# A hybrid decoder layer: small transfers on another queue, later gates, earlier reloads, and pairs that begin with a plain unit

## The chip, the cores and the metric

The kernel runs on one core of a Trainium2 chip. The metric is the device time of one execution in microseconds. The median of three runs before the change is 2062.15 us (2055.52 to 2067.89).

The core has a matrix engine (TensorE, PE in the profile), three engines for elementwise work (VectorE = DVE, ScalarE = ACT, GpSimd = POOL) and a queue engine (SyncE = SP). Transfers between memory and the chip are issued by SP, ACT or POOL, each in the order of its own instructions.

## The reference

A batch of 1, 256 tokens and 2048 features pass through one decoder layer in float32:

```python
hn = rmsnorm(h, norm_mix_w)
q, k, v, g_ret, xr, yr, g_a, g_b = split(hn @ w_in)
ret_out = silu(g_ret) * head_groupnorm(chunkwise_retention(rotary(q), rotary(k) * 128**-0.5, v))
rnn_out = gelu(yr) * rg_lru(causal_dwconv(xr), w_a, w_x, lam)
merged = sigmoid(g_a) * (ret_out @ w_proj_ret) + sigmoid(g_b) * (rnn_out @ w_proj_rnn)
h = h + merged @ w_mix_out
h = h + cross_attention(rmsnorm(h), rmsnorm(mem), w_q, w_k, w_v, w_o)   # 256 memory tokens, 4 heads of 512
u = causal_dwconv(rmsnorm(h) @ ffn_w_up)                                # 2 x 5632
h = h + (silu(gate) * val) @ ffn_w_down
return rmsnorm(h, final_norm_w)
```

## The kernel before

**Products.** Every float32 operand is split into a high and a low half that TensorE multiplies exactly, and a product is the sum of three: high by high, low by high, high by low. Activations are kept split (tiles `s`, in groups of two feature tiles); weights are split as they arrive.

**The weight stream.** `weight_plan` lists the blocks of 512 columns in the order of their use; `entry_units` cuts each into units of 4 feature tiles by 512 columns (1 MB). `prefetch` handles one unit: a transfer from `wall` into one of five `raw` buffers on SP (L261), a copy to `hi` by ScalarE (L282, 1.9 us), a subtraction into `lo` by VectorE (L283, 2.3 us). The generator `units` keeps two units split ahead of the matmuls (AHEAD).

**Single blocks and pairs.** `gemm_t` (L342) and `gemm_n` (L352 to L354) multiply one block. `pair_products` (L380 to L383) multiplies two blocks at once, and for the first eight of its 16 feature tiles it uses seven products where eight would be needed (a Strassen-like scheme): seven units `q1` to `q7` of 12 matmuls, and four plain units `p` of 24. Some `q` units work on sums of weights: "add" units are made by an accumulating transfer on POOL into a raw buffer that is already there (L263), a "sum" unit by a VectorE addition of two raw buffers (L287, at `q5`). Their other operand may be `ss`, sums of activations (`sums`, L479 to L485). Order of a pair's units:

```python
q1  p(8-11)  q3  p(12-15)  q5  q2  q6  p(8-11)  p(12-15)  q7  q4
```

where `p(8-11)` reads feature tiles 8 to 11, `p(12-15)` the last four, and `q1` four of the first eight. There are 16 pairs.

**Order of the work.** `later(n, fn)` puts `fn` off until n + 1 more units have been emitted. A framework schedules the program: each engine's instructions are put in an order from priority (the order of the program) and a simulated time at which they are ready, and run in that order.

**Kept tiles.** `Kept` stores finished tiles of `ret`, `rnn` and `qs` (256 KB each, eight of each) to memory and loads them back at the first `[i]`, splitting them, both on POOL (L711, L718). `Pairs` loads tiles of `x_t` and `mem_t` on SP (L607), up to two ahead; `ms` is the memory. `hkept` holds the residual during attention (4 x 512 KB, POOL, L1041 and L1137).

**The stages that the change touches.** (a) `recurrent` runs four times, each with two single blocks, and puts `recur` off: its gates (16 TensorE matmuls at L854 and 16 ScalarE functions for four tiles) in one go after the next unit, then `weigh`, `drive`, `scan`. (b) Three gate pairs (O_GA, O_GA, O_GB) follow; the last recurrence falls into the first. `ret` and `rnn` come back around there. (c) Attention: two pairs on `xa_w_q` whose results are transposed and stored in `qs` by `keep`; two pairs on `xa_w_k`, whose results `turn_key` transposes before `softmax`, two heads each; one pair on `xa_w_v` and two singles, each followed by `attend`. Memory rows `ms[0..3]` are asked for in the second `xa_w_q` pair, `ms[4..7]` in the first two units of the first `xa_w_k` pair; queries `qs[i]` in `turn_key`. (d) The feed-forward: 11 blocks in parts of 4, 4, 3; the first two parts end with two pairs each on `ffn_w_down`, whose 16 feature tiles are the part's hidden tiles, the last of them finished just before.

Of the kernel before, what the change touches and what calls it, by code (L numbers as in the profile page):

```python
# [19 lines left out]
NT = D // P  # L20
# [7 lines left out]
BW = 512  # L28
KC = 4
# [34 lines left out]
def weight_plan():  # L64

    w0 = "w_in"
    plan = []
    for g in range(2):
        for c in (O_Q, O_K):
            plan += [(w0, 0, NT, c + g * BW), (w0, 0, NT, O_V + g * 1024 + (c == O_K) * BW)]  # L70
        plan += [(w0, 0, NT, O_G + g * 1024 + b * BW) for b in range(2)]
    for b in range(4):
        plan += [(w0, 0, NT, c + b * BW) for c in (O_XR, O_YR)]
    for w, c, pairs in ((w0, O_GA, (0, 2)), (w0, O_GB, (0,)), ("w_proj_ret", 0, (0, 2))):
        plan += [(w, 0, NT, c + b * BW, c + (b + 1) * BW) for b in pairs]
        if len(pairs) == 1:
            plan += [(w, 0, NT, c + b * BW) for b in (2, 3)]
    plan += [("w_proj_rnn", 0, NT, b * BW) for b in range(4)]
    plan += residual_plan("w_mix_out")
    plan += [(w, 0, NT, b * BW, (b + 1) * BW) for w in ("xa_w_q", "xa_w_k") for b in (0, 2)]  # L80
    plan += residual_plan("xa_w_v")
    plan += residual_plan("xa_w_o")
    b0 = 0
    for nb_ in FF_PARTS:
        for b in range(b0, b0 + nb_):
            plan += [("ffn_w_up", 0, NT, c + b * BW) for c in (0, FF)]
        if nb_ == 4:
            plan += [("ffn_w_down", b0 * BW, NT, b * BW, (b + 1) * BW) for b in (0, 2)]
        else:
            plan += [("ffn_w_down", b0 * BW, 4 * nb_, b * BW) for b in range(4)]  # L90
        b0 += nb_
    return plan
# [19 lines left out]


def entry_units(e):

    w, row, nk, cols = e[0], e[1], e[2], e[3:]
    if len(cols) == 1:
        return [("p", None, "new", (w, tuple(row + (k + i) * P for i in range(KC)), cols[0])) for k in range(0, nk, KC)]
    out = []
    for kind, slot, a in PAIR_UNITS:  # L120
        if kind == "p":
            out.append((kind, slot, "new", (w, tuple(row + (a[1] + i) * P for i in range(KC)), cols[a[0]])))
        elif a[0] == "sum":
            out.append((kind, slot, "sum", None))
        else:
            out.append((kind, slot, a[0], (w, tuple(row + (2 * i + a[1]) * P for i in range(KC)), cols[a[2]])))
    return out
# [23 lines left out]
def hybrid_layer(  # L151
# [215 lines left out]
    def pair_products(w, row, st, ss, c0, c1, out):  # L367
# [17 lines left out]
        names = {"q1": "x", "q2": "y", "q3": "r", "q4": "u", "q5": "z", "q6": "x", "q7": "x"}  # L385
        for kind, parts in units(w, row, NT, c0, c1):
            if kind == "p":
# [316 lines left out]
    class Kept(list):  # L704
# [4 lines left out]
        def store(self, t):  # L709

            pool.dma_start(out=self.rows[self.stored], in_=t)  # L711
            self.stored += 1

        def __getitem__(self, i):
            while len(self) <= i:
                assert len(self) < self.stored
                t = tmp("kt")
                pool.dma_start(out=t, in_=self.rows[len(self)])  # L718
                self.append(split_pair(t, self.scale))
                if self.summed and len(self) <= KC:  # L720
                    self.sums.append(sums(t, self.scale))
# [125 lines left out]
    def recur(b, rgw, xr, gl):  # L847
        aa, tt_, ti = big([P, 4, S], s="aa"), big([P, 4, S], s="tt"), big([P, 4, S], s="ti")
        for j in range(4):
            t = 4 * b + j  # L850
# [34 lines left out]

        for n, fn in zip((0, 1, 2) if b < 3 else (6, 11, 17), (weigh, drive, scan)):
            later(n, fn)
# [32 lines left out]
    def sum_x(i):  # L920

        t = tmp("xt")
        pool.dma_start(out=t, in_=x_t[:, 2 * i : 2 * i + 2, :])
        for j in range(2):
# [115 lines left out]
    for b in range(4):  # L1040
        pool.dma_start(out=hkept[b], in_=hrow[b])  # L1041

# [48 lines left out]
    for b in (0, 2):  # L1091
        if b == 2:
            for i in range(KC):
                later(2 + 2 * i, lambda i=i: ms[i])
        for i, o in enumerate(pair_out("xa_w_q", h1s, h1s_sums, b * BW)):
            for pr in range(2):
                later(2 * i + pr, lambda o=o, pr=pr: keep(o, pr, qs))
    for i in range(KC):
        later(i // 2, lambda i=i: ms[KC + i])

    def turn_key(b, o, pr, ks):
        for t in transposed(o[:, :, pr * S : (pr + 1) * S]):
            ks.append(split_pair(t))
        qs[2 * b + pr]
        if pr == 1:
            later(1, lambda: softmax([qs[2 * b], qs[2 * b + 1]], ks))

    for b in (0, 2):
        for i, o in enumerate(pair_out("xa_w_k", ms, ms.sums, b * BW, rsms[0])):
            ks = []  # L1110
            for pr in range(2):
                later(3 * i + pr, lambda b=b + i, o=o, pr=pr, ks=ks: turn_key(b, o, pr, ks))
    osp, osp_sums = [], []
# [19 lines left out]
    for i, o in enumerate(pair_out("xa_w_v", ms, ms.sums, 0)):  # L1133
        later(3 * i, lambda b=i, o=o: attend(b, split_rows(o, rsms[0])))
    hrow = [big([P, 2, BW], s="nat") for _ in range(4)]
    for i in range(4):
        pool.dma_start(out=hrow[i], in_=hkept[i])  # L1137
    for b in (2, 3):
# [141 lines left out]
```

## Time and profile before

| | |
|---|---|
| median of 3 runs | 2062.15 us |
| profiled execution, its time | 2058.05 us |
| its span, first to last instruction | 2056.2 us |
| busy: PE, DVE, ACT, POOL | 2018.2, 1496.6, 1128.1, 83.0 us |
| mean granted TensorE clock | 0.991 |
| bytes read and written | 431.45 MB, 10.49 MB |
| SP's queue, POOL's queue | 371.17 MB, 68.16 MB |

Times in views of the trace are microseconds from the start of the span. A row of a group gives line, engine, operation, tiles, count, busy time and idle time before it with what ended it. A wait "A <- B: t, n, m" says that A waited for B t us in all, n times, at most m. In the chain of waits, a row is what the end of the kernel hung on at that moment. A row of transfers ends with the median time from issue to landing.

### The profile page before, as it was taken

To read this page: it belongs to the slowest core of one execution; us is meant where nothing else is said; L and a number is where in the kernel's file an instruction comes from. 1 tells how busy PE (TensorE), PEld (TensorE's weight loads), DVE (VectorE), ACT (ScalarE), POOL (GpSimd) and SP (SyncE) were. 2 spreads that over 40 slices of the span, in tenths; PEclk is the share of its full clock that TensorE was granted. 3 is DMA by queue.
4 is the path that set the end of the run, shared out by engine and by line. 5 is a ranking of instruction groups with operands and counts; after the bars stand their busy time and mean duration, and the time that the engine had idled before them with its cause. 6 is when DMAs were issued, how large, how long until landed. Compare 5 with 4: busy or idle time off the path is not lost.

```text
span 2056.2 us, 24973 instructions
## 1 busy us (share of the span) xinstructions
PE 2018.2 (98%) x10120; PEld 1708.9 (83%) x10120; DVE 1496.6 (73%) x1535; ACT 1128.1 (55%) x1143; POOL 83.0 (4%) x120
## 2 busy tenths in 40 slices
PE   9999999999999999999899899999999999999998
PEld 8888888888788888888787788888878888788887
DVE  6747657988775776777776667578778687776765
ACT  6445447766565554565655555555454555454543
POOL 0000000000100000000100000000000000000000
PEclk9999999999999999999899999999999999999999
DMA  9554554565887775887967757555569555685552
GB/s 365 209 213 181 188 195 160 215 209 156 267 285 254 227 267 193 256 282 236 292 205 219 236 164 226 185 192 192 188 185 279 185 202 192 165 278 213 184 205 82
DMA packets 74403, 443.56 MB, mean 216 GB/s; under 512 B 8496, under 2 KB 13232, under 8 KB 25008
## 3 DMA queue, kind: packets, MB, share of 16 engines
q1 hardware_dynamic: 60544, 371.17, 48.8%
q0 software_dynamic: 12224, 68.16, 15.3%
q10 hardware_dynamic: 1520, 2.63, 0.4%
q8 instruction: 79, 1.29, 0.2%
q14 instruction: 36, 0.29, 0.0%
HBM read 431.45 MB, written 10.49 MB: 215 GB/s over the span
## 4 chain that ended last, share of the span: by engine, by line
PE 84%; DVE 5%; DMA 5%; ACT 3%; issue 2%; POOL 0%; SPq 0%; POOLq 0%; DVEq 0%; ACTq 0%
PE acc L342 34%; PE acc L354 8%; PE acc L352 8%; PE acc L353 8%; PE acc L383 8%; PE acc L380 8%; PE acc L382 8%; DVE lo L283 3%; DMA raw<-in_wall 2%; PE sm L496 2%; ACT hi L282 1%; DMA xt<-in_mem_t 1%; DMA kt<-qs 1%; PE sm L508 1%; DVE raw L287 0%
## 5 line engine op out<-in xcount | busy, mean ns | idle before, releaser
L283 DVE TENSOR_TENSOR lo<-raw,hi 128x2048 fp32r<-128x2048 f32 (+1 forms) x408 | 923.0, 2269 | 425.1 <-ACT hi L282 424.0
L282 ACT CAST hi<-raw 128x2048 fp32r<-128x2048 f32 (+1 forms) x406 | 769.7, 1901 | 672.3 <-PE acc L353 175.8
L342 PE MATMUL acc<-s,hi 128*128 128x512 f32 x2176 | 520.0, 392 | 1.5 <-DVE hi L280 0.9
L342 PEld LDWEIGHTS acc<-s,hi 128*128 128x128 f32 x2176 | 402.5, 189 | 81.6 <-issue 1.4
L352 PE MATMUL acc<-hi,s 128*128 128x512 f32 (+1 forms) x760 | 292.6, 385 | 0.0
L354 PE MATMUL acc<-lo,s 128*128 128x512 f32 (+1 forms) x760 | 291.4, 383 | 0.0
L353 PE MATMUL acc<-hi,s 128*128 128x512 f32 (+1 forms) x760 | 291.1, 383 | 0.0
L342 PEld LDWEIGHTS acc<-s,lo 128*128 128x128 f32 x2176 | 278.4, 192 | 11.0 <-DVE lo L283 1.9
L380 PE MATMUL acc<-hi,s 128*128 128x512 f32 x704 | 279.2, 397 | 7.3 <-ACT hi L282 4.3
L342 PE MATMUL acc<-s,lo 128*128 128x256 f32 x2176 | 284.3, 284 | 1.1 <-DVE lo L283 1.1
L383 PE MATMUL acc<-lo,s 128*128 128x512 f32 x704 | 278.3, 395 | 5.2 <-DVE lo L283 5.0
L382 PE MATMUL acc<-hi,s 128*128 128x512 f32 x704 | 278.1, 395 | 1.1 <-DVE s L553 1.1
L354 PEld LDWEIGHTS acc<-lo,s 128*128 128x128 f32 x760 | 142.9, 188 | 28.2 <-DVE lo L283 0.2
L353 PEld LDWEIGHTS acc<-hi,s 128*128 128x128 f32 x760 | 143.0, 188 | 27.2 <-DVE s L530 0.2
L352 PEld LDWEIGHTS acc<-hi,s 128*128 128x128 f32 x760 | 143.0, 188 | 27.0 <-ACT s L529 0.3
L380 PEld LDWEIGHTS acc<-hi,s 128*128 128x128 f32 x704 | 133.9, 190 | 37.4 <-ACT hi L282 6.2
L383 PEld LDWEIGHTS acc<-lo,s 128*128 128x128 f32 x704 | 134.0, 190 | 36.9 <-DVE lo L283 9.6
L382 PEld LDWEIGHTS acc<-hi,s 128*128 128x128 f32 x704 | 134.0, 190 | 30.0 <-DVE s L553 1.9
L380 PE MATMUL acc<-hi,ss 128*128 128x512 f32 x256 | 101.7, 397 | 0.9 <-ACT o L434 0.4
L383 PE MATMUL acc<-lo,ss 128*128 128x512 f32 x256 | 100.5, 392 | 0.1
L382 PE MATMUL acc<-hi,ss 128*128 128x512 f32 x256 | 99.9, 390 | 0.0
L263 POOL DMA_DIRECT2D raw<-in_wall x48 | 41.9, 873 | 1086.3 <-DVE lo L283 765.8
(243 smaller groups left out, 1422.5 us busy)
## 6 DMA issues: line engine op xcount, KB each, us to landing
raw<-in_wall SPq DMA_DIRECT2D x337, 1024.0 KB, 4.9
raw<-in_wall POOLq DMA_DIRECT2D x48, 1024.0 KB, 9.3
raw<-in_wall SPq DMA_DIRECT2D x5, 512.0 KB, 8.5
nat<-in_x ACTq DMA_DIRECT2D x4, 512.0 KB, 10.5
ret<-hd POOLq DMA_DIRECT2D x8, 256.0 KB, 6.5
rnn<-rn POOLq DMA_DIRECT2D x8, 256.0 KB, 4.2
kt<-ret POOLq DMA_DIRECT2D x8, 256.0 KB, 8.3
kt<-rnn POOLq DMA_DIRECT2D x8, 256.0 KB, 5.5
```

What stands on the lines that cost most here:

```text
L263: pool.dma_start(out=raw, in_=src, accum_op=ALU.add)
L282: act.copy(hi[:, a:b], raw[:, a:b])
L283: dve.tensor_tensor(out=lo[:, a:b], in0=raw[:, a:b], in1=hi[:, a:b].bitcast(F32), op=ALU.subtract)
L342: pe.matmul(a, part, sx, start=k == 0 and t == 0, stop=k == nk - 1 and t == 0, skip_group_check=True)
L352: pe.matmul(o, h, hi, start=start, stop=False)
L353: pe.matmul(o, l, hi, start=False, stop=False)
L354: pe.matmul(o, h, lo, start=False, stop=stop)
L380: pe.matmul(o[0], h, hi, start=o[1] not in begun, stop=False, skip_group_check=True)
L382: pe.matmul(o[0], l, hi, start=False, stop=False, skip_group_check=True)
L383: pe.matmul(o[0], h, lo, start=False, stop=kk == KC - 1, skip_group_check=True)
L496: pe.matmul(o, a, b, start=start and i == 0, stop=stop and i == 2, skip_group_check=True)
L508: pe.transpose(t[:, j, tt * P : (tt + 1) * P], rows[:, tt, k + j * P : k + (j + 1) * P], ident)
```

## The change

- The stores and loads of `Kept`, the `x_t` tiles of `sum_x`, and `hkept`'s stores and loads are issued by SP in place of POOL. The accumulating weight transfers stay on POOL.
- `recur` puts its four gate tiles off singly: two after the first unit, two after the second; `weigh`, `drive`, `scan` follow two units later than before in the first three recurrences.
- Three of the 16 pairs carry a flag in the plan: the first O_GA pair, and the first `ffn_w_down` pair of each of the two full parts. A flagged pair takes its units in the order `p(8-11) q1 p(12-15) q3 q2 q5 q6 p p q7 q4`; the weight stream follows.
- `ms[0]` and `ms[1]` are asked for in the first `xa_w_q` pair, `ms[2..7]` in the second.
- `qs[0..3]` are asked for after units 5, 7, 9 and 11 of the first `xa_w_k` pair, `qs[4..7]` in the second, and no longer in `turn_key`.
- `keep`, `turn_key` and the first two `attend` come one unit later.

```diff
-        plan += [(w, 0, NT, c + b * BW, c + (b + 1) * BW) for b in pairs]
+        plan += [(w, 0, NT, c + b * BW, c + (b + 1) * BW) + (True,) * (c == O_GA and b == 0) for b in pairs]
...
-            plan += [("ffn_w_down", b0 * BW, NT, b * BW, (b + 1) * BW) for b in (0, 2)]
+            plan += [("ffn_w_down", b0 * BW, NT, b * BW, (b + 1) * BW) + (True,) * (b == 0) for b in (0, 2)]
...
+PLAIN_FIRST = [PAIR_UNITS[i] for i in (1, 0, 3, 2, 5, 4, 6, 7, 8, 9, 10)]
...
-    w, row, nk, cols = e[0], e[1], e[2], e[3:]
+    w, row, nk, cols = e[0], e[1], e[2], e[3:5]
...
-    for kind, slot, a in PAIR_UNITS:
+    for kind, slot, a in PLAIN_FIRST if e[5:] else PAIR_UNITS:
...
-        for kind, parts in units(w, row, NT, c0, c1):
+        e = (w, row, NT, c0, c1)
+        for kind, parts in units(*e, *plan[gemms[0]][5:]):
...
-            pool.dma_start(out=self.rows[self.stored], in_=t)
+            sp.dma_start(out=self.rows[self.stored], in_=t)
...
-                pool.dma_start(out=t, in_=self.rows[len(self)])
+                sp.dma_start(out=t, in_=self.rows[len(self)])
...
-        for j in range(4):
+
+        def gates(j):
...
-        for n, fn in zip((0, 1, 2) if b < 3 else (6, 11, 17), (weigh, drive, scan)):
+        for j in range(4):
+            later(j // 2, lambda j=j: gates(j))
+        for n, fn in zip((2, 3, 4) if b < 3 else (6, 11, 17), (weigh, drive, scan)):
...
-        pool.dma_start(out=t, in_=x_t[:, 2 * i : 2 * i + 2, :])
+        sp.dma_start(out=t, in_=x_t[:, 2 * i : 2 * i + 2, :])
...
-        pool.dma_start(out=hkept[b], in_=hrow[b])
+        sp.dma_start(out=hkept[b], in_=hrow[b])
...
-        if b == 2:
-            for i in range(KC):
-                later(2 + 2 * i, lambda i=i: ms[i])
+        for i in range(KC):
+            if b == 0 and i < 2:
+                later(5 + 4 * i, lambda i=i: ms[i])
+            elif b == 2:
+                later(2 * i, lambda i=i: ms[i])
+                later(9 + i // 2, lambda i=i: ms[KC + i])
...
-                later(2 * i + pr, lambda o=o, pr=pr: keep(o, pr, qs))
-    for i in range(KC):
-        later(i // 2, lambda i=i: ms[KC + i])
+                later(1 + 2 * i + pr, lambda o=o, pr=pr: keep(o, pr, qs))
...
-        qs[2 * b + pr]
...
+        for i in range(KC):
+            later(4 + 2 * i, lambda i=i: qs[2 * b + i])
...
-                later(3 * i + pr, lambda b=b + i, o=o, pr=pr, ks=ks: turn_key(b, o, pr, ks))
+                later(1 + 3 * i + pr, lambda b=b + i, o=o, pr=pr, ks=ks: turn_key(b, o, pr, ks))
...
-        later(3 * i, lambda b=i, o=o: attend(b, split_rows(o, rsms[0])))
+        later(1 + 3 * i, lambda b=i, o=o: attend(b, split_rows(o, rsms[0])))
...
-        pool.dma_start(out=hrow[i], in_=hkept[i])
+        sp.dma_start(out=hrow[i], in_=hkept[i])
```

## The prediction

> **What bounds the kernel now.** I read the page first: which engine is full, and what is left of the span.
>
> ```profile
> span 2056.2 us, 24973 instructions
> PE 2018.2 (98%) x10120; PEld 1708.9 (83%) x10120; DVE 1496.6 (73%) x1535; ACT 1128.1 (55%) x1143; POOL 83.0 (4%) x120
> PEclk9999999999999999999899999999999999999999
> ```
>
> TensorE is busy 98% of the span, so no edit beside it can shorten the work. What can go is the time in which it stands or runs at a lower granted clock. To find that I cut the span into stages. A stage is one weight block (a "single", or a "pair" of blocks made of 11 units and 180 matmuls); its bounds come from the matmul counts in the timeline. The view by windows gives length, PE busy and the matmul count of each. Columns: window, length, busy and count of PE, PEld, DVE, ACT, POOL, then the granted clock, DMA share, GB/s.
>
> ```profile
> 334.90:361.00 26.10, 26.10 (x148) 22.74 (x146) 19.29 (x24) 20.73 (x34) 1.64 (x3) 1.00 0.58 211
> 361.00:384.10 23.10, 22.53 (x130) 19.66 (x129) 23.10 (x33) 13.29 (x16) 1.63 (x3) 1.00 0.61 226
> 410.20:433.40 23.20, 22.55 (x130) 19.76 (x129) 21.62 (x32) 12.46 (x15) 1.65 (x3) 1.00 0.68 238
> 481.90:529.30 47.40, 45.63 (x198) 36.38 (x197) 37.64 (x34) 36.66 (x41) 3.98 (x6) 1.00 0.65 200
> 529.30:576.00 46.70, 43.13 (x181) 34.69 (x181) 36.41 (x34) 25.46 (x19) 5.36 (x8) 0.96 0.87 266
> 660.50:701.40 40.90, 40.90 (x181) 33.72 (x180) 28.42 (x16) 24.83 (x19) 1.96 (x3) 1.00 0.72 223
> 920.90:963.90 43.00, 42.62 (x190) 34.30 (x189) 30.43 (x22) 25.39 (x24) 3.92 (x5) 1.00 0.74 234
> 963.90:1007.70 43.80, 43.15 (x198) 35.22 (x197) 37.04 (x39) 31.28 (x34) 4.04 (x7) 1.00 0.94 288
> 1007.70:1061.30 53.60, 48.83 (x197) 38.52 (x196) 35.71 (x28) 29.75 (x30) 7.27 (x11) 0.87 0.79 249
> 1061.30:1118.40 57.10, 52.34 (x253) 43.77 (x252) 38.73 (x37) 30.45 (x34) 4.87 (x8) 0.94 0.68 203
> 1118.40:1176.20 57.80, 52.33 (x253) 43.66 (x252) 39.24 (x37) 30.62 (x35) 4.43 (x7) 0.94 0.74 225
> 1228.80:1272.90 44.10, 44.06 (x205) 36.27 (x204) 31.15 (x20) 24.17 (x17) 1.71 (x2) 1.00 0.67 204
> 1498.90:1543.60 44.70, 42.05 (x182) 33.39 (x181) 36.35 (x32) 24.51 (x21) 1.71 (x2) 1.00 0.66 201
> 1762.50:1807.00 44.50, 42.21 (x183) 33.47 (x183) 36.36 (x32) 24.61 (x21) 1.75 (x2) 1.00 0.66 201
> ```
> The chain of waits has the undisturbed single (start us, us, what):
> ```profile
> 53.35 22.22 PE acc L342 x128
> ```
>
> The measure of a pair that nothing disturbs is 40.9 us (660.50); a unit of it is 12 matmuls, 2.7 us, and a plain unit 24 matmuls, 5.4 us. The pair at 1228.80 has 24 more small matmuls and takes 3.2 us more, so one costs 0.13. Its neighbours are measured against that:
>
> - Pairs on xa_w_k and xa_w_v at 1061.30 and 1118.40: 72 small ones, 9.4 us. Lost: 57.1 - 40.9 - 9.4 = **6.8**, and **7.5**.
> - First xa_w_k pair at 1007.70: 16 small ones, 2.1. Lost: 53.6 - 40.9 - 2.1 = **10.6**.
> - The xa_w_q pairs: 43.0 - 40.9 - 1.0 = 1.1, and 43.8 - 40.9 - 2.1 = 0.8.
> - First two gate pairs at 481.90 and 529.30: 94.1 less 81.8, less the recurrence's 16 gate matmuls (26.1 - 22.2 = 3.9, first row). Lost: **8.4**.
> - First ffn_w_down pairs: **3.8** and **3.6**.
> - Two stages behind recurrences (361.00, 410.20): 0.9 and 1.0.
>
> About 44 us in all: no change to the waits can bring more. Now what ended last in the worst of them, from the chain of waits, SP's timeline and VectorE's timeline:
>
> ```profile
> 1011.14 9.59 DMA xt<-in_mem_t
> ...
> 1083.26 0.56 POOL raw L263
> 1083.82 12.95 DMA kt<-qs
> 1096.80 0.63 ACT s L526
> ...
> 1140.99 13.62 DMA kt<-qs
> ```
> ```profile
> 1001.12 9.93 SPq L261 DMA_DIRECT2D raw<-in_wall  x3
> 1011.14 2.22 SPq L607 DMA_DIRECT2D xt<-in_mem_t  x3
> ```
> ```profile
> 529.08 0.29 DVE L479 TENSOR_TENSOR sm<-kt 128x128 f32<-128x128 f32 x1 [1.59 <-DMA kt<-ret]
> 534.32 0.29 DVE L479 TENSOR_TENSOR sm<-kt 128x128 f32<-128x128 f32 x1 [2.14 <-DMA kt<-ret]
> ...
> 1509.64 0.69 DVE L530 SCALAR_TENSOR_TENSOR s<-fo,s 128x512 fp32r<-128x512 f32 x1
> ...
> 1512.44 0.69 DVE L530 SCALAR_TENSOR_TENSOR s<-fo,s 128x512 fp32r<-128x512 f32 x1
> ```
>
> At 1083.8 a query reload leaves GpSimd right behind an accumulating weight load, lands 13 us later, and softmax's matmuls wait for its split; the same at 1141.0. At 1001-1011 SyncE's queue stood before three weight loads, and the last three memory rows left only then. The clock adds to each: it is granted at half for 13.6 us there and for 6.8 us behind the first query wait.
>
> ```profile
> 1013.60:1027.20 13.60, 10.79 (x28) 7.80 (x29) 6.67 (x10) 5.25 (x12) 3.85 (x7) 0.50 1.00 368
> 1095.50:1102.30 6.80, 4.83 (x20) 4.51 (x21) 4.41 (x5) 4.70 (x4) 0.00 (x0) 0.50 0.45 178
> ```
>
> **The change, part by part.**
>
> *Queries a block ahead: -12.3.* Before, a query was asked for two or three units ahead of its softmax (turn_key after unit 1 + 3i + pr, softmax two units on): 8 to 14 us against 13 us of transfer. Now query i of the pair of heads is asked for after unit 5 + 2i of the pair before, the last with unit 11, and softmax of the head that needs it comes after units 5 and 8 of the next. That leaves eight units or more, 30 us. The splits (0.63 us on ScalarE, about as much on VectorE) move with it, four into the pair at 1007.70, whose VectorE loses four memory splits in exchange. I leave 1.0 us per pair, as in the xa_w_q pairs, which have no such wait: -5.8 - 6.5 = -12.3. Bounds: 0 if the reload still lands late, -14.3 if all goes.
>
> *Memory rows earlier, transposes one unit later: -6.1.* The last four memory pairs were asked for after units 1 and 2 of the xa_w_k pair that uses the first of them in its unit 2. Now it is units 10 and 11 of the pair before: 5.4 and 8.2 us earlier; two more go to the first xa_w_q pair. The transfers then land at 1013 to 1015 instead of 1020.7, against 1010.4 when unit 2 begins. 3 to 5 us of wait stay, with a little of the low clock: I leave 4.5 of 10.6. Transposes of a result (keep, turn_key, attend) come one unit later, so that they no longer stand right behind VectorE's last add. Bounds: 0, and -9.6 with 1.0 left.
>
> *First gate pair begins plain, gates two tiles per unit: -2.9, and -0.9 at the recurrences.* The plain unit gives the splits 5.4 us in place of 2.7 at the start, and ScalarE gets eight of its 16 gate functions a unit later. But the two waits of VectorE above (1.59 and 2.14) are for kept rows, which the change doesn't bring earlier; I leave 5.5 of 8.4 and half of 1.9. Bounds: 0 and -7.4; 0 and -1.9.
>
> *First ffn_w_down pairs begin plain: +2.0.* Old order: q1, plain 8-11, q3, plain 12-15, so the plain unit that reads the last two hidden tiles begins 2.7 + 5.4 + 2.7 = 10.9 us in. New order: plain, q1, plain: 8.2 us in, at 1507.0. Those tiles' splits end at 1510.3 and 1513.1 (rows at 1509.64 and 1512.44), and VectorE's timeline shows no gap from 1500 to there. The wait is 3.3, then four to six matmuls, then 1.4: 4.7 against the 3.8 and 3.6 lost now, as the later stalls of the pair are taken in by it: +0.9 and +1.1. Bounds: -2.8 each if the scheduler puts those splits first, +4 each if the clock falls too.
>
> *Small transfers on SyncE's queue: 0.* 60 move: 8 stores and 8 loads each of ret, rnn and qs, 4 of x_t, 8 of hkept. Waits and landings in the profile:
>
> ```profile
> SPq L261 <- DVE lo L283: 1690.6, 312, 19.8
> ```
> ```profile
> xt<-in_mem_t SPq DMA_DIRECT2D x8, 256.0 KB, 10.1
> kt<-qs POOLq DMA_DIRECT2D x8, 256.0 KB, 12.1
> xt<-in_x_t SPq DMA_DIRECT2D x7, 256.0 KB, 7.9
> xt<-in_x_t POOLq DMA_DIRECT2D x4, 256.0 KB, 5.1
> ```
>
> SyncE issues in order and waits most of the span for VectorE to free a raw buffer. A store that waits for VectorE stands in the same order as VectorE's own instructions, so it adds little; a load waits for the weight loads ahead. GpSimd keeps the 48 accumulating loads and loses what stood before them. The cover is the lead of two split units before the matmuls, 5.4 us or more. The price without it is the second rival's. Bounds: that rival, and -3.7 (1.59 + 2.14) if kept rows land in time.
>
> The Trainium skill, "SBUF — State Buffer", section "SBUF: two separate sides", says that transfers issued from GpSimd starve for descriptors while VectorE runs certain copies, and that SP's run at full speed. By it those 3.7 us would go, and the sum be 3.7 lower. The rows don't bear it out: the same x_t tile took 5.1 us from GpSimd and 7.9 from SyncE. I go by the rows.
>
> **Sum.** -12.3 - 6.1 - 2.9 - 0.9 + 2.0 = -20.2. The profiled execution took 2058.05 us, 1.85 over its span: 2037.9. The median of the three runs, 2062.15, lies 4.1 above it (2055.52 to 2067.89); I add half of that: **2040**.
>
> **The rivals.**
>
> 1. *The queries aren't early in fact.* They are asked for on SyncE, where a load goes behind weight loads that wait for buffers: the memory rows stood 9.9 us so. If the reloads are held until the pair that uses them, -12.3 falls away: -7.9, that is 2050, with the median's 2 about 2052; up to 2060 if the other steps do half. For it: the SyncE rows above. Against: 30 us of lead against 10 of waiting and 10 of landing.
>
> 2. *Slower: VectorE stands before rows that SyncE brings late.* VectorE runs in order; a split of a kept row set before a weight's lo half holds that half, and TensorE with it. This is what the pair at 1007.70 shows: memory rows on SyncE, 10.6 lost. 16 reloads of ret and rnn fall into the three gate pairs and after, 8 of qs into the pairs at 1007.70 and 1061.30. If the gate pairs each lose 10.6 (31.8 against 8.4 now: +23.4) and the three attention pairs too (31.8 against 24.9: +6.9), with +2.0 and -0.9: +31.4, 2091. It decides as soon as a small load lands more than two units (5.4 us) after its place in VectorE's order. The Trainium skill, "DMA: Bandwidth & Descriptors", section "Anatomy of one DMA — SWDGE (gpsimd) path", has the rule behind it: a wait is held on the issuing sequencer, before dispatch. SyncE's 1690.6 us of waiting agree.
>
> 3. *More goes.* All bounds on the good side but the ffn ones: -14.3 - 9.6 - 7.4 - 1.9 = -33.2, 2025, with the median's 2: 2027; to 2018 with the ffn gain and the kept rows.
>
> **How the numbers follow.** A measurement of this kernel tells about 0.5%, 10.3 us, from no change: faster is below 2051.8, slower above 2072.5. Forecast (2030 to 2051) 0.55; rival 3 (2018 to 2030) 0.08; rival 1 (2052 to 2060, same) 0.17; rival 2 (2073 and more) 0.20. Faster 0.63, same 0.17, slower 0.20. The range takes in the first three: 2018 to 2060.
>
> **What would show it.** Right: kt<-qs gone from the chain of waits, the pairs after the first xa_w_k pair at 51 to 52 us with the clock at 1.00; the first xa_w_k pair at 47 to 49; the first ffn_w_down pairs at 45 to 46 with TensorE waiting in the second plain unit for s of L530. Wrong: VectorE's sums or splits waiting for kt rows in the gate pairs, weight loads on SyncE that reach hi late in pairs, or query reloads still issued in the pair that uses them.

## The result, and the profile after

The changed kernel takes **2055.33 us** (median of 20 runs, 2048.99 to 2060.42), the kernel before 2059.71 us in its 20 runs. The ratio is 0.9974, with a 95% interval of 0.9963 to 0.9984. So it is faster, but by 4.4 us in place of the 20 that were forecast, and by less than the 0.5% that counted as faster. The time lies inside the forecast's range of 2018 to 2060, but only in the part that was given to the first rival. The profiled execution took 2055.16 us against 2058.05, 2.9 less; all sums below are made between these two.

The head of the page after. GpSimd has lost 60 of its 120 instructions; nothing else in it tells what happened.

```profile
span 2053.3 us, 24938 instructions
PE 2014.6 (98%) x10120; PEld 1706.2 (83%) x10120; DVE 1495.3 (73%) x1535; ACT 1127.5 (55%) x1143; POOL 50.0 (2%) x60
```

The view by windows, cut at the same stages as before (columns as in the prediction). In order: the two `xa_w_k` pairs, the `xa_w_v` pair; the first `ffn_w_down` pair of each full part.

```profile
1002.80:1050.90 48.10, 43.83 (x198) 35.01 (x198) 35.90 (x25) 29.89 (x28) 2.61 (x3) 1.00 0.85 262
1050.90:1101.50 50.60, 50.30 (x254) 41.64 (x253) 37.39 (x35) 26.21 (x28) 2.60 (x3) 1.00 0.78 239
1101.50:1157.80 56.30, 52.50 (x253) 43.67 (x252) 39.11 (x36) 32.50 (x35) 2.62 (x3) 0.94 0.72 227
1480.30:1533.20 52.90, 47.03 (x183) 36.14 (x182) 37.56 (x34) 24.64 (x21) 2.54 (x3) 0.90 0.59 169
1751.90:1803.90 52.00, 44.82 (x182) 34.40 (x181) 36.66 (x32) 24.41 (x21) 1.72 (x2) 0.97 0.58 166
```

Stage by stage against before, by the exact starts in the timelines:

| stage | before | after | difference | forecast |
|---|---|---|---|---|
| recurrences 2 to 4, six stages | 146.9 | 144.3 | -2.6 | -0.9 |
| three gate pairs | 135.1 | 133.0 | -2.1 | -2.9 |
| first `xa_w_k` pair | 53.65 | 48.10 | -5.5 | -6.1 |
| second `xa_w_k`, `xa_w_v` pair | 114.9 | 107.0 | -7.9 | -12.3 |
| first `ffn_w_down` pair, twice | 44.72, 44.44 | 52.88, 52.01 | **+15.7** | +2.0 |

The first `ffn_w_down` pair began at 1498.88 and now begins at 1480.27: up to there the change has won 18.6 us, where the forecast's terms for these stages add to 22.2. Then the two flagged `ffn_w_down` pairs give back 15.7. 18.6 - 15.7 = 2.9, the whole difference of the two profiled executions.

What TensorE waits for in the first of these two pairs, before and then after (from its timelines, all rows with a wait; in brackets the wait, and whose result ended it):

```profile
1511.77 0.50 PE L380 MATMUL acc<-hi,s 128*128 128x512 f32 x1 [0.88 <-ACT hi L282]
1523.60 0.51 PE L380 MATMUL acc<-hi,s 128*128 128x512 f32 x1 [0.74 <-ACT hi L282]
1541.20 0.50 PE L383 MATMUL acc<-lo,s 128*128 128x512 f32 x1 [0.94 <-DVE lo L283]
```
```profile
1489.23 0.49 PE L383 MATMUL acc<-hi,s 128*128 128x512 f32 x1 [0.61 <-ACT s L533]
1491.54 0.50 PE L383 MATMUL acc<-hi,s 128*128 128x512 f32 x1 [1.82 <-ACT hi L285]
1494.82 0.79 PE L383 MATMUL acc<-hi,s 128*128 128x512 f32 x1 [0.27 <-ACT s L533]
1496.30 0.79 PE L386 MATMUL acc<-lo,s 128*128 128x512 f32 x1 [0.69 <-DVE lo L286]
1511.03 0.50 PE L383 MATMUL acc<-hi,ss 128*128 128x512 f32 x1 [1.39 <-ACT hi L285]
1512.83 0.59 PE L383 MATMUL acc<-hi,s 128*128 128x512 f32 x1 [1.07 <-ACT hi L285]
```

Some rows of VectorE and ScalarE in the same stretch, after:

```profile
1491.55 0.68 DVE L534 SCALAR_TENSOR_TENSOR s<-fo,s 128x512 fp32r<-128x512 f32 x1
1493.96 2.28 DVE L286 TENSOR_TENSOR lo<-raw,hi 128x2048 fp32r<-128x2048 f32 x1
1496.16 0.68 DVE L534 SCALAR_TENSOR_TENSOR s<-fo,s 128x512 fp32r<-128x512 f32 x1
1506.69 2.29 DVE L290 TENSOR_TENSOR raw<-raw,raw 128x2048 f32<-128x2048 f32 x1
```
```profile
1502.42 1.91 ACT L285 CAST hi<-raw 128x2048 fp32r<-128x2048 f32 x1 [7.66 <-PE acc L385]
```

There are two stretches of waiting. The **first**, 1489 to 1496, is the one that was forecast: `p(12-15)`, now the third unit, stands before the last hidden tiles are split (VectorE's rows of L534 at 1491.55 and 1496.16). Its four waits add to 3.4 us, where 4.7 were forecast. Two of them are for weights of `q2`. The framework has put matmuls of `q2` among those of `p(12-15)`: from 1489.23 to 1502.4 the timeline shows 29 matmuls on plain `s`, five more than `p(12-15)` has, and the twelve of `q3`, on `ss`, behind them. So `q2`'s splits are wanted early too, and its `lo` (1493.96) stands on VectorE between pieces of hidden tiles. The **second**, 1509 to 1513, 2.5 us, wasn't forecast: the `hi` of the sixth unit, `q5`, can be written only when the third unit's buffer is free, since there are three (`PART_BUFS`), and ScalarE idles 7.66 us for that. VectorE's sum for `q6` (L290) comes behind it, at 1506.69, and the `hi` of `q6` behind the sum. In the old order `q5` is the fifth unit, and `q2` stands between it and `q6`.

And the clock falls, which it didn't do in this pair before: 6.8 us at half clock follow the first stretch and 3.4 the second, by the view by windows:

```profile
1492.60:1499.40 6.80, 5.84 (x13) 3.76 (x12) 4.24 (x5) 0.63 (x1) 0.00 (x0) 0.50 0.27 88
1513.10:1516.50 3.40, 3.40 (x9) 2.61 (x9) 3.40 (x3) 1.48 (x1) 0.87 (x1) 0.50 1.12 231
```

Waits of TensorE in this pair add to 5.9 us, and half of the busy time at half clock, (5.84 + 3.40)/2, to 4.6: 10.5 of the 12.0 by which the pair stands over 40.9. Before, the waits added to 2.6 of the 3.8 lost, at full clock. So of the 8.2 us that the pair has grown by, 3.3 are waits and 4.6 are the clock.

In the `xa_w_v` pair (from 1101.48) a query reload is still late. The chain of waits, and SP's timeline, after:

```profile
1095.73 6.34 DMA kt<-qs
```
```profile
1081.90 13.78 SPq L264 DMA_DIRECT2D raw<-in_wall  x3
1095.73 0.90 SPq L722 DMA_DIRECT2D kt<-qs  x2
```

SP stood 13.8 us before three weight loads in the pair before, and the last two reloads, asked for a block ahead in the program, left only then. They landed at 1102, just inside the pair that uses them, whose granted clock in the view by windows is 0.94.

### The profile page after: what moved, and what is told of

It reads as the page before. It is cut to its first block, busy times and chain, and to the rows that moved or that the text cites. A ratio compares the mean times of both kernels' runs of the same rounds, so it can differ in the third digit from the quotient of the medians.

```text
span 2053.3 us, 24938 instructions
## 1 busy us (share of the span) xinstructions
PE 2014.6 (98%) x10120; PEld 1706.2 (83%) x10120; DVE 1495.3 (73%) x1535; ACT 1127.5 (55%) x1143; POOL 50.0 (2%) x60
## 3 DMA queue, kind: packets, MB, share of 16 engines
q1 hardware_dynamic: 69184, 389.00, 50.9%
## 4 chain that ended last, share of the span: by engine, by line
PE 89%; DMA 4%; DVE 4%; ACT 2%; issue 1%; SPq 0%; POOL 0%; POOLq 0%; DVEq 0%; ACTq 0%
PE acc L345 36%; PE acc L386 8%; PE acc L383 8%; PE acc L385 8%; PE acc L357 8%; PE acc L355 8%; PE acc L356 8%; DVE lo L286 2%; DMA kt<-qs 2%; DMA raw<-in_wall 2%; PE sm L500 1%; ACT hi L285 1%; PE sm L512 1%; PE sm L859 1%; DMA xt<-in_mem_t 1%
## 5 line engine op out<-in xcount | busy, mean ns | idle before, releaser
L383 PE MATMUL acc<-hi,s 128*128 128x512 f32 x704 | 280.3, 398 | 14.7 <-ACT hi L285 7.3
L383 PEld LDWEIGHTS acc<-hi,s 128*128 128x128 f32 x704 | 133.8, 190 | 46.9 <-ACT hi L285 9.6
L522 ACT COPY c<-acc 128x512 f32<-128x512 f32 x68 | 39.1, 578 | 72.0 <-PE acc L345 71.9
```

The costliest lines, as they stand in the source:

```text
L383: pe.matmul(o[0], h, hi, start=o[1] not in begun, stop=False, skip_group_check=True)
L522: act.copy(c, a[:, :, S:BW])
```

## The experiments

The theory after the result: *all that the change wins up to the feed-forward is real, and the flagged order of the `ffn_w_down` pairs takes most of it back.* The rival: the feed-forward pairs only receive a delay that some other part (SP's queue, say) brings, and would be as long in the old order. Where one run of a kernel is given, its stage lengths carry the reading, as far as the spread told below the table allows. Line numbers are each kernel's own.

**Old order in the feed-forward alone** (`ffn_old`, on which most other experiments stand).

```diff
-            plan += [("ffn_w_down", ...) + (True,) * (b == 0) for b in (0, 2)]
+            plan += [("ffn_w_down", ...) for b in (0, 2)]
```

> The changed kernel, but with the two feed-forward pairs in the old order of units. Theory A (the order of the units costs these pairs 8.2 and 7.6 us and the rest of the change brings 18.6): both pairs come back to 44 to 45 us, the stages ahead of them stay, and the time falls by 15 to 16 us to about 2040, 0.990 of the kernel before. Theory B (the pairs pay for transfers and reloads that moved to other places, not for their order): the pairs stay at 51 to 53 and the time at 2053 to 2057.

2039.43 us (median of 4), ratio to before 0.9882 (0.9859 to 0.9906). The view by windows of the two pairs:

```profile
1480.60:1524.80 44.20, 42.10 (x183) 33.43 (x181) 36.35 (x32) 24.57 (x21) 1.76 (x2) 1.00 0.67 203
1743.70:1788.10 44.40, 42.14 (x183) 33.41 (x182) 36.36 (x32) 24.56 (x21) 1.73 (x2) 1.00 0.66 202
```

They are back at 44, with the clock at 1.00, and start where they do after (1480.6 against 1480.3). The 15.9 us between the medians fit the pairs' 8.7 + 7.6 = 16.3.

**The flagged order in the feed-forward alone**, put into the kernel before.

```diff
+            plan += [("ffn_w_down", ...) + (True,) * (b == 0) for b in (0, 2)]     # all else as before
```

> The kernel before, with the plain-first order in the two feed-forward pairs alone. Theory A (the order alone costs): the pairs at 1499 and 1762 us grow from 44.7 and 44.5 to 52 to 53, and the time rises by 15 to 16 us, to about 2075, 1.0075 of the kernel before. Theory B (it costs only together with the moved transfers): the pairs stay under 46, the time within 4 us of the kernel before. The size that I predicted for this step was +2.

2080.91 us (median of 4), ratio 1.0078 (1.0048 to 1.0108): slower, and by more than expected, with pairs of 54.1 and 53.2 us in place of 44.7 and 44.4 and the clock at 0.91 and 0.90 in them. With the first experiment this is shown from both sides: the flags cost 16 to 18 us in these two pairs, whatever the rest.

**Which part of the order costs.** The flagged order differs from the old one in three things: the pair begins with a plain unit, the second plain unit comes third, and `q2` stands before `q5`. Two kernels try one thing in each of the two pairs.

```diff
 # orders_xy, first part:  p q1 q3 p q5 q2 ...     (plain start alone)
 # orders_xy, second part: q1 p q3 p q2 q5 ...     (swap alone)
 # orders_z,  first part:  p q1 p q3 q5 q2 ...     (both plain units early, no swap)
 # orders_z,  second part: q1 p p q3 q5 q2 ...     (second plain unit early alone); first gate pair in the old order
```

> The changed kernel with two other orders in the feed-forward pairs. First one: plain, q1, q3, plain, q5, q2 (begins plain, the rest as of old). Second one: q1, plain, q3, plain, q2, q5 (only q2 and q5 changed over). Theory A1 (the second plain unit comes before the last hidden tiles are split): the first pair 44 to 45, the second 44 to 46. Theory A2 (q5 now stands right before the sum unit q6, whose weights need q5's halves, an addition and two more halves): first pair 44 to 45, second 51 to 53. Both at once: first 44 to 45, second 46 to 49.

> The changed kernel with the first gate pair in the old order, and two other orders in the feed-forward pairs. First one: plain, q1, plain, q3, q5, q2 (as changed, but q5 and q2 in the old order). Second one: q1, plain, plain, q3, q5, q2 (second plain unit early, start as of old). Theory A1 (last hidden tiles): both pairs 49 to 53. Theory A2 (q5 right before q6): both 44 to 46. Both at once: both 47 to 50. Gate pairs: if the plain start helps them, they together grow by 3 us or more over the changed kernel's 133.0 (three pairs); if not, they stay within 2 us.

2038.51 and 2039.35 us (one run each). The windows of the four pairs, of `orders_xy` and then of `orders_z`:

```profile
1479.20:1524.20 45.00, 42.10 (x182) 33.52 (x181) 36.43 (x32) 24.45 (x21) 1.76 (x2) 1.00 0.66 192
1743.10:1787.10 44.00, 42.18 (x182) 33.42 (x181) 36.43 (x32) 24.56 (x21) 1.73 (x2) 1.00 0.67 204
```
```profile
1477.60:1524.40 46.80, 43.13 (x183) 34.42 (x182) 37.38 (x34) 24.76 (x21) 2.55 (x3) 0.96 0.66 193
1743.10:1788.10 45.00, 41.63 (x182) 33.55 (x181) 36.90 (x33) 24.98 (x20) 1.84 (x3) 1.00 0.66 202
```

The ten kernels with the old order in both pairs have pairs of 43.8 to 46.3 us, so neither the plain start (45.0) nor the swap (44.0) costs anything that can be read alone. The early second plain unit costs 2.6 and 0.7 us against `ffn_old`, of which only the first stands out, and barely. That is less than the theories of the late hidden tiles had (47 to 53), and near the 2.0 of the forecast. Only the swap and the early plain unit together cost 8. TensorE's waits in the first pair of `orders_z`, all of them:

```profile
1486.53 0.50 PE L385 MATMUL acc<-hi,s 128*128 128x512 f32 x1 [0.61 <-ACT s L535]
1489.59 0.53 PE L387 MATMUL acc<-hi,s 128*128 128x512 f32 x1 [2.56 <-DVE s L536]
1493.59 0.51 PE L388 MATMUL acc<-lo,ss 128*128 128x512 f32 x1 [0.49 <-DVE lo L288]
```

Without the swap the first stretch is as long, 3.7 us against 3.4 after, and one step of 3.4 us at half clock follows it in place of two; but nothing waits behind it. There the prediction's sentence holds: the later stalls are taken in. The swap brings the second stretch back. That `q2`'s matmuls stand in the first stretch doesn't make its waits longer. In `orders_z` the first gate pair has the old order, and the three gate pairs take 130.7 us against 130.8 in `ffn_old`: the plain start there brings nothing that can be read.

**Is it the late hidden tiles?** In this kernel the first pair of each full part multiplies tiles 12 to 15 by the split of tiles 0 to 3, so part of that product is another one.

```diff
-                pair_add("ffn_w_down", b0 * BW, hid, hid_sums, ...)
+                pair_add("ffn_w_down", b0 * BW, hid[:6] + hid[:2] if b == 0 else hid, hid_sums, ...)
```

> The changed kernel as it is, but the first pair of each full feed-forward part multiplies its feature tiles 12 to 15 with the split of tiles 0 to 3 in place of their own, which was made long before; part of the product is thereby another one, all work is still done. Theory H (the second plain unit waits for the last hidden tiles; sixth in the new order is q5, whose halves can only be made when the third unit gives its buffers back, and behind it stands the sum unit: so the second wait of 4 us is a consequence of the first): both waits go, the pairs fall from 52.9 and 52.0 to 41 to 45. Rival D (two independent waits): 46 to 49. Rival E (weights, not hidden tiles, are late): 51 to 53.

2040.61 us (one run):

```profile
1481.20:1526.20 45.00, 42.86 (x182) 34.73 (x181) 36.81 (x33) 24.45 (x20) 1.98 (x3) 0.96 0.68 195
1745.00:1789.40 44.40, 41.76 (x183) 33.48 (x181) 36.44 (x32) 24.31 (x21) 1.73 (x2) 1.00 0.67 194
```

The first stretch of waits is gone, and with it 7.9 and 7.6 us. The second stays, against the theory's words, though the lengths are those it gave: 1.07 + 1.07 us in place of 1.39 + 1.07, so it belongs to the order itself, and costs about what the old order loses elsewhere in the pair. With `orders_z` the first pair adds up: waits of 3.7 us without the swap and 2.1 without the late tiles make 5.8, against 5.9 with both. Either one takes the place of the old order's own waits (2.0 in `ffn_old`) and so costs little; both together cost in full, with three steps at half clock where each alone has one. So the loss needs the wait for the last hidden tiles, and the swap behind it.

**Is the second wait curable by a later `q6`?** Here the last two `p` units come before `q6`, so that the sum has time (the orders are written out).

```diff
-PLAIN_FIRST = p q1 p q3 q2 q5 q6 p p q7 q4
+PLAIN_FIRST = p q1 p q3 q2 q5 p p q6 q7 q4
```

> The changed kernel with one more change in its plain-first order: the sum unit q6 comes behind the two last plain units, so that q5 doesn't stand right before it. Theory C (the feed-forward pairs lose 8 us by two waits, one on the last hidden tiles at the second plain unit and one on the sum unit behind q5): the second goes, and the pairs fall from 52.9 and 52.0 to 47 to 49. Theory D (the first wait alone sets the loss): they stay at 51 to 53.

2071.97 us (one run), pairs of 58.3 and 60.4 us: the idea failed, and neither theory had such lengths. Rows of TensorE's, SP's and ScalarE's timelines of this kernel:

```profile
1512.11 0.50 PE L385 MATMUL acc<-hi,ss 128*128 128x512 f32 x1 [1.96 <-ACT hi L287]
```
```profile
1497.82 16.99 SPq L266 DMA_DIRECT2D raw<-in_wall  x3
```
```profile
1520.96 1.91 ACT L287 CAST hi<-raw 128x2048 fp32r<-128x2048 f32 x1 [8.90 <-DMA raw<-in_wall]
```

The wait for `q6` didn't go: two matmuls behind `q5`, at 1512.11, TensorE again stands for the `hi` of `q6` (the next on `ss`), since the framework puts its matmuls early all the same. And a wait on the stream itself comes on top. SP stands 17 us before three loads; ScalarE then waits 8.9 us for a weight, and TensorE 3.8 us at 1531, in the second pair 6.1. A sum's raw buffers are held until its unit is split, and there are five; the rows fit that, but no run tries it. Whether the pair would fall without the second stretch isn't shown by this kernel.

**The other parts, undone one by one in `ffn_old`.** The table gives the stages that they touch, by exact starts in the timelines; each experiment follows it.

| kernel | three gate pairs | 2nd `xa_w_q` | 1st `xa_w_k` | 2nd `xa_w_k` | `xa_w_v` | these four |
|---|---|---|---|---|---|---|
| before | 135.1 | 43.8 | 53.7 | 57.1 | 57.8 | 212.3 |
| after | 133.0 | 44.7 | 48.1 | 50.6 | 56.4 | 199.8 |
| `ffn_old` | 130.8 | 45.2 | 47.8 | 50.8 | 56.0 | 199.8 |
| `small_pool` | 136.2 | 45.6 | 53.3 | 49.7 | 49.7 | 198.3 |
| `gates_once` | 140.8 | 50.7 | 48.3 | 49.6 | 50.9 | 199.5 |
| `queries_late` | 133.8 | 44.8 | 45.8 | 54.2 | 50.5 | 195.1 |
| `pool_queries_late` | 135.6 | 44.4 | 45.8 | 52.2 | 50.7 | 193.0 |
| `query_loads_pool` | 132.4 | 44.9 | 51.4 | 50.5 | 51.2 | 197.9 |
| `memory_late` | 130.5 | 43.2 | 55.2 | 49.7 | 50.6 | 198.6 |
| `transposes_early` | 132.1 | 44.9 | 54.6 | 57.6 | 49.5 | 206.7 |
| `mixed_queues` | 131.8 | 44.6 | 47.6 | 51.2 | 53.7 | 197.0 |

How far these columns can be read is told by kernels that are the same up to the feed-forward. After, `ffn_old`, `orders_xy`, `hidden_early` and `sum_later` run the same instructions in the same order on every engine up to their first `ffn_w_down` pair. Yet their gate pairs take 130.8 to 135.0 us, the second `xa_w_q` pair 44.7 to 47.1, the first `xa_w_k` pair 47.8 to 50.6, the `xa_w_v` pair 51.4 to 56.4; the four together 196.5 to 199.8. Before and `ffn_only`, alike in the same way, take 135.1 and 140.4 in the gate pairs. So a difference of five us in one column carries nothing. Steadier are the sum of the four and the six recurrence stages, 144.3 us in all five.

*Small transfers back on GpSimd:*

```diff
-            sp.dma_start(out=self.rows[self.stored], in_=t)
+            pool.dma_start(out=self.rows[self.stored], in_=t)     # and so the loads, x_t and hkept
```

> The changed kernel with the old feed-forward order (2039.4 us), and the 60 small transfers back on GpSimd's queue. My predicted step was 0: 2036 to 2043, stages within 1 us. Theory S (SyncE's queue holds the last query reloads behind weight loads, and the xa_w_v pair waits for them): that pair falls from 56.0 to 51 to 53 us, and the time by 2 to 5. Theory G (the move itself brought the gain in the gate pairs, since stores waiting on GpSimd no longer stand before the accumulating weight loads): the three gate pairs grow from 130.8 to 134 us or more.

2044.15 us (median of 4), ratio 0.9914 (0.9897 to 0.9931), against 0.9882 (0.9859 to 0.9906): 4.7 us slower by the medians, with intervals that overlap. By stages it is 6.7 us longer in the second gate pair and 5.5 in the first `xa_w_k` pair, and 6.3 shorter in the `xa_w_v` pair. Only the first follows the queue: the second gate pair takes 48.3 and 47.8 us in the two kernels with all small transfers on GpSimd (`small_pool`, `pool_queries_late`), and 41.0 to 42.4 in all with later gates and these loads on SP. The other two lie near the spread, and `pool_queries_late` has a first `xa_w_k` pair of 45.8. The gate pair, in rows of the chain of waits of `small_pool`:

```profile
545.74 1.40 POOL kt L722 x2
550.82 14.72 DMA raw<-in_wall
```

Here the order is the other way round than in the prediction's example: two loads of kept rows have gone out, the next accumulating weight load goes out behind them and takes 14.7 us, where the median of such loads is 9.4. The `hi` that needs it begins at 565.63, and TensorE stands for it. That the loads ahead of it made it slow is likely, but not shown.

*Queries asked for in `turn_key` again, on SP; and the same with all small transfers on GpSimd:*

```diff
             ks.append(split_pair(t))
+        qs[2 * b + pr]
...
-        for i in range(KC):
-            later(4 + 2 * i, lambda i=i: qs[2 * b + i])
```

> As the first of these, transfers on SyncE, but the queries asked for in turn_key as before. Theory Q (the reload's early request brings the gain): the second xa_w_k pair goes from 50.8 to 57 us and the xa_w_v pair from 56.0 to 58 or more; the time 2045 to 2050. Rival (the move to SyncE or the transposes one unit later did it): both pairs stay within 1 us, 2039.

> The same base, with small transfers on GpSimd's queue and queries asked for in turn_key: of the query step only the one unit's delay of transposes is left. Theory Q (the early request is what freed the second xa_w_k pair and the xa_w_v pair on GpSimd's queue, 49.7 us each there): the two go back to 55 to 58 us each. Theory T (the later transposes did it): they stay at 49 to 52.

2039.07 and 2035.42 us (one run each). The early request brings nothing that can be read: without it the four pairs are no longer than with it, 195.1 against 199.8. In the second kernel queries go out as late as before and on the old queue, and yet the two pairs that lost 6.8 and 7.5 before take 52.2 and 50.7. Something else had cured them.

*Transposes one unit earlier, as before:*

```diff
-                later(1 + 2 * i + pr, lambda o=o, pr=pr: keep(o, pr, qs))
+                later(2 * i + pr, lambda o=o, pr=pr: keep(o, pr, qs))     # turn_key and attend likewise
```

> The changed kernel with the old feed-forward order (2039.4 us), and the transposes of keep, turn_key and attend after the same unit as before, one earlier. Theory T (the later transposes bring the 12.6 us that the four xa_w_q, xa_w_k and xa_w_v pairs gained whether queries and memory rows are early or late): the four pairs grow from 199.8 to 208 to 212 us, the time to 2047 to 2051. Rival V (the queue and the early requests bring it, each one enough): the four stay within 2 us, time 2038 to 2041.

2046.87 us (one run), just short of the theory's range; the four pairs take 206.7 in place of 199.8. Windows of the two `xa_w_k` pairs:

```profile
1002.70:1057.30 54.60, 46.84 (x196) 36.64 (x197) 36.72 (x25) 29.75 (x27) 3.41 (x4) 0.94 0.79 241
1057.30:1114.90 57.60, 52.28 (x253) 43.33 (x252) 38.95 (x37) 30.44 (x33) 2.33 (x4) 0.94 0.70 201
```

Both are as long as before, 53.7 and 57.1, with the queries and the memory rows still asked for early. Together the two take 110.8 to 112.2 us in the three kernels without the delay (this one, before, `ffn_only`) and 98.0 to 104.8 in the thirteen with it. So the unit of delay is what shortened them: it puts the transposes, the softmax behind them and their wants a unit later. The `xa_w_v` pair, whose `attend` is early here too, is 49.5, so the delay isn't what shortens that one. The prediction had the delay as half a sentence in the memory term.

*Memory rows as before:*

```diff
-        for i in range(KC): ...              # ms[0..7] in the two xa_w_q pairs
+        if b == 2:
+            for i in range(KC):
+                later(2 + 2 * i, lambda i=i: ms[i])
+    for i in range(KC):
+        later(i // 2, lambda i=i: ms[KC + i])
```

> As the first of these, transfers on SyncE, but the memory rows asked for as before (four in the second xa_w_q pair, four in the first xa_w_k pair); transposes still one unit later. Theory M (the earlier request brings the 5.6 us): the first xa_w_k pair goes from 47.8 to 52 to 54 us. Rival (the later transposes did it): it stays under 49.5.

2036.72 us (one run). The first `xa_w_k` pair is 7.4 us longer, as the theory has it, but the other three are 8.6 us shorter: nothing in sum that can be read.

*All four gate tiles at once:*

```diff
-            later(j // 2, lambda j=j: gates(j))
-        for n, fn in zip((2, 3, 4) if b < 3 ...
+            gates(j)
+        for n, fn in zip((0, 1, 2) if b < 3 ...
```

> As the first of these, transfers on SyncE, but all four gate tiles of a recurrence in one go, as before. Theory R (spreading brings it): the six stages of the second to fourth recurrence, up to the first gate pair, grow from 144.3 to 146 to 147 us, and the first two gate pairs from 88.3 by 2 to 5. Rival (the move of stores and of x_t tiles did it): both stay within 0.5.

2051.44 us (one run), 12.0 more than `ffn_old`: the recurrences take 147.0 us in place of 144.3, the gate pairs 140.8 in place of 130.8, the first two of them 99.9 in place of 88.3. Rows with waits in the first gate pair, of VectorE and TensorE:

```profile
529.86 0.29 DVE L483 TENSOR_TENSOR sm<-kt 128x128 f32<-128x128 f32 x1 [7.42 <-DMA kt<-ret]
```
```profile
512.04 0.79 PE L383 MATMUL acc<-hi,s 128*128 128x512 f32 x1 [4.27 <-ACT hi L285]
532.41 0.50 PE L386 MATMUL acc<-lo,s 128*128 128x512 f32 x1 [1.92 <-DVE lo L286]
```

The mechanism of the prediction's second rival is seen here: VectorE stands 7.4 us for a kept row, a weight's `lo` comes behind, and TensorE stands 1.9 us for that. But the longest wait of the pair is another, 4.3 us for a `hi`. And VectorE stands for a kept row with GpSimd's queue too, in the trace of `ffn_only`, which has the order of the kernel before there, and whose gate pairs take 140.4:

```profile
536.14 0.29 DVE L483 TENSOR_TENSOR sm<-kt 128x128 f32<-128x128 f32 x1 [4.16 <-DMA kt<-ret]
```

So the recurrences' 2.7 us are the later gates' (all traces with them have 144.3, the three without 146.9 to 147.0). Of the gate pairs' 10, five are within the spread, and that the gates at once are worse on SP's queue than on GpSimd's isn't shown: 140.8 against 135.1 and 140.4. Before with SP's queue alone wasn't run.

*Only the query loads on GpSimd; and a mixture (`ret`, `rnn` and `x_t` on SP, `qs` and `hkept` on GpSimd, queries asked for late), the best of each by the table:*

```diff
-                sp.dma_start(out=t, in_=self.rows[len(self)])
+                (sp if self.scale or self.summed else pool).dma_start(out=t, in_=self.rows[len(self)])
```

> The same base, with all small transfers on SyncE except the eight query reloads, which stay on GpSimd. Theory S (SyncE brings the gate pairs' and the first xa_w_k pair's gain, but holds the query reloads behind weight loads): gate pairs 130 to 132 us, first xa_w_k pair 47 to 49, the next two 49.5 to 51 each; time 2031 to 2035. Rival (these stalls only move from one pair to another): the four attention pairs stay at 197 to 201 in all, time 2037 to 2041.

> What the earlier runs point to: old feed-forward order, gates two per unit, transposes one unit later, memory rows early; ret, rnn and x_t on SyncE, qs and the kept residual on GpSimd, queries asked for in turn_key. Theory (each stage keeps the better of its two values): gate pairs 130 to 132, the four attention pairs 192 to 195, time 2029 to 2034, 2 to 4 per mille below the version with all on SyncE (2039.4). Rival (stalls move on): 2036 to 2041.

2038.58 us (median of 4), ratio 0.9879 (0.9862 to 0.9895), and 2037.93 (median of 4), ratio 0.9889 (0.9873 to 0.9906). The `xa_w_v` pair comes down by 4.8 and 2.3 us, and other pairs go up in part. Both are `ffn_old` again within the intervals. About 2038 us, 1.1% under before, is the best median that was found, and undoing the two `ffn_w_down` flags alone reaches it.

## Why the prediction was wrong, point by point

- **First `ffn_w_down` pairs, +2.0: the step that failed.** Measured +8.2 and +7.6. The mechanism was named (`p(12-15)` stands before the last hidden tiles) and its wait wasn't taken too small: 3.4 and 4.5 us, where 4.7 were forecast. What failed is the sentence that "the later stalls of the pair are taken in by it": 2.5 us of waits came behind it in each pair, at `q6`. And the clock, which stood only in the bound of +4 each, fell in both: in the first pair it cost 4.6 us, the larger part, in the second 1.7. Without the swap the sentence holds, and the cost is 2.6 and 0.7. The prediction counted units up to `p(12-15)`; it did not ask what the swap of `q2` and `q5` does to the buffers and to the sum behind it.
- **Queries a block ahead, -12.3.** Those two pairs gained 7.9, but not by this step: undone, it costs nothing. Of the 7.9, 6.5 are in the second `xa_w_k` pair, and the later transposes gave them. The `xa_w_v` pair gained 1.4, less than its spread of five. The quoted rows were true, a reload did end last; but a want that comes a unit later cures that as well as a request that comes a block sooner.
- **The first rival** was half right. Its reloads are held on SP as it said, 13.8 us, and land in the `xa_w_v` pair. The time lies where it put it (2050 to 2060), but that is luck: the loss is in the feed-forward, for which it has only the forecast's +2.0.
- **Memory rows and transposes, -6.1.** The pair came out at 48.1, inside the 47 to 49 forecast, and the term at -5.5. So the number was right, but by luck: in the sum the memory part is worth nothing that can be read, and the transposes' part, undone, costs 6.9 us over the four pairs, more than the whole term.
- **Gates and first gate pair, -0.9 and -2.9.** In sum near (-4.7 against -3.8). The recurrences' -2.6 is steady over all traces and lies beyond the bound of -1.9, which was taken from two of the six stages; the gate pairs' -2.1 is inside their spread, and the plain start brings nothing that can be read.
- **SyncE's queue, 0.** At most 4.7 us of gain, by intervals that overlap; by stages only the second gate pair follows the queue. The Trainium skill, "SBUF — State Buffer", section "SBUF: two separate sides", has transfers from SP run at full speed where those from GpSimd starve behind certain copies of VectorE. The landing times, rows below (after, then `small_pool`), are mixed: the stores of `rnn` gain, 2.1 us against 3.5; those of `ret` don't, 7.3 against 6.8; `kt<-ret` takes 8.6 on SP and 9.2 on GpSimd. The four x_t tiles, in the view from 300 to 500 us, take 5.4 and 4.3. The prediction had 7.9 against 5.1 for these tiles; but the 7.9 is the median of seven loads in the first 13 us of the kernel, and the 5.1 of four between 345 and 414. What stands ahead in the queue weighs more: 13.8 us before the last two reloads.

```profile
rnn<-rn SPq DMA_DIRECT2D x8, 256.0 KB, 2.1
ret<-hd SPq DMA_DIRECT2D x8, 256.0 KB, 7.3
kt<-ret SPq DMA_DIRECT2D x8, 256.0 KB, 8.6
```
```profile
rnn<-rn POOLq DMA_DIRECT2D x8, 256.0 KB, 3.5
ret<-hd POOLq DMA_DIRECT2D x8, 256.0 KB, 6.8
kt<-ret POOLq DMA_DIRECT2D x8, 256.0 KB, 9.2
```

Open: why the waits in the gate and attention stages move from pair to pair. The order of instructions alone doesn't decide it, since the five kernels named under the table have the same order there and differ by up to 5 us in a pair. So it is left to times that differ between runs; which of them, no run shows. Open too is what shortened the `xa_w_v` pair from 57.8 us to 49.5 to 56.4: no single step, undone, brings it back.

## What to carry to other kernels

When the units of a product are put in another order, follow for each of them three things: the operand that it reads and when it is ready, the split buffer that it takes and which unit must end first, and the raw buffers that a sum keeps; a wait that takes the place of an old one costs little, two waits where one was cost in full, and the clock can add nearly as much again. A stall that a late load ends can be cured on either end, and a try of each alone tells which edit did it. Before a stage of one trace is read as the work of an edit, look how much that stage differs between kernels that are the same up to it: here up to 5 us in one pair, and next to nothing in the recurrences.

## What the runs showed of the hardware

In these traces TensorE's granted clock changes in steps of 3.4 us, and falls to half for the step behind one in which TensorE was busy for less than about half. The view by windows, after, on these steps:

```profile
1489.20:1492.60 3.40, 1.53 (x4) 0.78 (x5) 3.40 (x7) 2.29 (x2) 0.00 (x0) 1.00 0.00 0
1492.60:1496.00 3.40, 2.74 (x6) 1.28 (x4) 3.40 (x4) 0.63 (x1) 0.00 (x0) 0.50 0.00 0
1042.10:1045.50 3.40, 1.68 (x8) 1.06 (x6) 2.81 (x2) 3.40 (x6) 0.00 (x0) 1.00 1.02 424
1765.70:1769.10 3.40, 1.67 (x6) 1.20 (x7) 2.77 (x2) 0.63 (x1) 0.00 (x0) 1.00 0.06 19
1779.40:1782.80 3.40, 2.01 (x10) 1.34 (x8) 1.38 (x2) 1.98 (x2) 0.86 (x1) 1.00 0.00 0
1782.80:1786.20 3.40, 2.33 (x9) 1.50 (x10) 3.40 (x2) 3.40 (x2) 0.75 (x1) 1.00 1.03 169
```

Busy for 1.53 us, the next step is at half clock, and so is the one behind 1.67 (1769.1 to 1772.5); behind steps at full clock with 1.68 and more it is not. The other traces put the bound between 1.5 and 1.8: in `sum_later` a step with 1.51 (from 1803.5) is followed by full clock, in `query_loads_pool` one with 1.77 (from 1003.3) by half. At half clock the bound is another one: 2.74 us busy from 1492.6 on, and the next step is at half again; 2.96 in `gates_once` (from 511.6), and the next is at full. The last two rows are the second pair's wait before `q6`: TensorE loses as much there as at 1509 in the first pair, but the wait falls across a step's border, and the clock holds. So a wait of 2 us may cost 2 us or nearly 4 by where it falls. The Trainium skill, "TensorE: Matmul & The Clock Gate", section "HAM oscillation — how this bites in real kernels", gives as the rule that TensorE shouldn't stand for more than some 3.4 us. This trace doesn't agree: in the first `ffn_w_down` pair the longest single wait before the fall was 1.82 us, so shorter ones are enough.
